# Opening loads on two queues, and the bias products moved behind the fourth slice of a hybrid decoder layer

## The chip, the core and the metric

The kernel is one program on one core of a Trainium2 chip. The core has five engines with instruction streams of their own: TensorE (PE in the profile) multiplies, VectorE (DVE) and ScalarE (ACT) work elementwise, GpSimd (POOL) helps with copies, and SyncE (SP) mostly issues transfers. Transfers are moved by 16 DMA engines; SP, ACT and POOL can each issue them. The metric is the device time in microseconds (us) of one execution, as the median of several.

## What is computed

One layer of a decoder for 256 tokens of width 1024, all in float32. The parts that matter here, cut from the reference and shortened:

```python
h = jnp.einsum('bsd,de->bse', x, w_in[l])
qa, ka, va, za, qb, kb, vb, zb, ga, gb = _split_cols(h)
ya = swa_sink_attention(qa, ka, va, sinks[l], table_a) * jax.nn.silu(za)   # window 128
yb = moba_attention(qb, kb, vb, table_b) * jax.nn.silu(zb)                 # one block of 256
...
bias = rel_table.astype(jnp.float32)[t5_bucket(dist)]     # added to the attention logits
...
merged = sigmoid(ga + b) * (ya @ w_out_a) + sigmoid(gb + b) * (yb @ w_out_b)
x = layer_norm(DN_ALPHA * x + merged @ w_out, ln_gamma[l], ln_beta[l])
```

Each of the 16 heads adds to its logits a bias that depends only on the distance of query and key. The distance is put into one of 32 buckets, and the bias is the entry of a 32x16 table for this bucket and head.

## The kernel before

**Products in two parts.** A float32 operand is split into a high part, rounded to the one-pass format `fp32r`, and the rest (`xh`, `xl` for the input, `wh`, `wl` for weights). A product is high by high, low by high and high by low. So each weight tile is loaded (`wraw`, SP's queue), rounded by ACT into `wh` (L138), subtracted by DVE into `wl` (L153), and used by PE. There are five `wraw` buffers, so a load waits until DVE has finished the `wl` of the tile five before it; a load also waits for the transfer issued eight before it to land.

**Stages.** PE first runs nine warm-up products on constants (L65). Then come the value projections in eight slices k = 0 to 7 of the contraction (L313 to L318): slice k needs 128 rows of the input (`xraw`, 128 KB) and 320 KB of `w_v`, and PE does 12 products of 320 columns with them: four with `wh` and `xh`, four with `wh` and `xl`, four with `wl` and `xh`. After the slices come the projection tiles of `w_t`, 512 KB each, called here t0, t1, t2 and so on: t0 is the keys of the first branch, t1 to t4 its queries, then the second branch, gates and output. A head pair's scores follow its queries: the logits stand in a PSUM bank, DVE adds the bias and takes the row's extreme (L235, L248), ACT takes exponentials (L250), DVE normalises (L263 to L270), and PE transposes and applies the values.

**The bias.** A product of the table (`tab`, 32 rows, each head's column repeated 16 times) with a 0/1 matrix (`oh`, 32 rows, which bucket each distance has) gives for 128 partitions the bias along all distances. There are two such products, one per branch (L323). DVE copies each in reversed order into `rvec` (L324), POOL writes it to a scratch `rd` in device memory (L325), and SP reads it back skewed, as `toep`, 16 transfers of 128 KB (L120), two of them ahead of each of the tiles t2, t3 and t4, and so on. In `rd` and `toep` the halves are the branches: the first eight transfers of `toep` need only the first write. The first products with the table stand after slice 0.

**What sets the order.** It is written by hand: a list `order` of tiles is walked by two cursors, `fetch` (the load and ACT's rounding) and `split` (DVE's subtraction), which run two and one tiles ahead of PE in the slices, and further later. Each engine, and each queue, works in program order. So whatever stands on SP behind a `toep` transfer waits until this can be issued.

Of the kernel before, what the change touches and what calls it, by code (L numbers as in the profile page):

```python
# [11 lines left out]
F32 = mybir.dt.float32  # L12
F32R = mybir.dt.float32r
BF16 = mybir.dt.bfloat16
AF = mybir.ActivationFunctionType
ALU = mybir.AluOpType

P = 128
# [4 lines left out]
NB = 32  # L23
# [5 lines left out]
RL = 384  # L29
# [17 lines left out]
def hybrid_layer(ctx: ExitStack, tc: tile.TileContext, xT, x2, w_t, w_v, w_a, w_b, w_o,  # L47
                 b_gate, sinks, table, onehot, gamma, beta, out):
    nc = tc.nc
    const = ctx.enter_context(tc.tile_pool(name="const", bufs=1))  # L50
    wp = ctx.enter_context(tc.tile_pool(name="wp", bufs=1))
    work = ctx.enter_context(tc.tile_pool(name="work", bufs=2))
# [6 lines left out]
    def bank(tag):  # L59
        return psum.tile([P, 512], F32, tag=tag, name=f"ps_{tag}", bufs=banks[tag])  # L60
# [6 lines left out]

    rvec = work.tile([P, 2, RL], F32, tag="pr_", name="rvec", bufs=4)
    nc.gpsimd.memset(rvec, NEG)
    tab = const.tile([NB, 2 * P], F32, name="tab")  # L70
    oh = work.tile([NB, RL], F32, tag="res", name="oh")
    nc.gpsimd.dma_start(tab, table)
    nc.gpsimd.dma_start(oh, onehot)
    sink = const.tile([P, 8], F32, name="sink")
    nc.gpsimd.dma_start(sink, sinks)
    bg = const.tile([P, 16], F32, name="bg")
    nc.gpsimd.dma_start(bg, b_gate)
    ident = const.tile([P, P], F32, name="ident")
    make_identity(nc, ident)
    nsink = const.tile([P, 8], F32, name="nsink")  # L80
    eps = const.tile([P, 1], F32, name="eps")
    nc.gpsimd.memset(eps, LN_EPS)
# [7 lines left out]
    xraw = const.tile([P, NK, S], F32, tag="x8", name="xraw")  # L90
    xh = const.tile([P, NK, S], F32R, name="xh")
# [18 lines left out]
    def quarters(w):  # L110
        return w.rearrange("p (a b) -> p a b", a=4)[:, :, :S]

    def fetch(kind, n):

        if kind == "r":

            for a in (2 * n, 2 * n + 1):
                src = bass.AP(tensor=rd.tensor, offset=rd.offset + (a // 8) * 16 * RW + (a % 8) * RL,
                              ap=[[RW + 8, 16], [1, 8], [1, S]])
                nc.sync.dma_start(toep[:, a, :], src)  # L120
            return
        if kind == "v":
            nc.sync.dma_start(xraw[:, n, :], xT[:, n, :])
            nc.scalar.activation(xh[:, n, :], xraw[:, n, :], AF.Copy)
        width = 640 if kind == "v" else 1024
        src = {"v": lambda: w_v[:, n, :], "t": lambda: w_t[n], "a": lambda: w_a[n], "b": lambda: w_b[n],
               "o": lambda: w_o[n * P:(n + 1) * P, :]}[kind]()
        raw = wp.tile([P, 1024], F32, tag="raw", name="wraw", bufs=RAWS)
        wh = wp.tile([P, 4 * OW], F32R, tag="wh", name="wh", bufs=8)
        parts = 2 if (kind, n) == ("v", 0) else 1  # L130
        cuts = [slice(i * width // parts, (i + 1) * width // parts) for i in range(parts)]
        for cut in cuts:
            nc.sync.dma_start(raw[:, cut], src[:, cut])
        if kind == "o":
            nc.scalar.activation(quarters(wh), raw.rearrange("p (a b) -> p a b", a=4), AF.Copy)
        else:
            for cut in cuts:
                nc.scalar.activation(wh[:, cut], raw[:, cut], AF.Copy)  # L138
        raws[kind, n] = raw, wh, width

    def split(kind, n):

        if kind == "r":
            return
        if kind == "v":
            nc.vector.tensor_sub(xl[:, n, :], xraw[:, n, :], xh[:, n, :].bitcast(F32))
        raw, wh, width = raws.pop((kind, n))
        wl = wp.tile([P, 4 * OW], F32R, tag="wl", name="wl", bufs=8)
        if kind == "o":
            nc.vector.tensor_sub(quarters(wl), raw.rearrange("p (a b) -> p a b", a=4), quarters(wh).bitcast(F32))  # L150
            nc.vector.tensor_reduce(sums[:, n:n + 1], raw[:, 3 * S:], axis=mybir.AxisListType.X, op=ALU.add)
        else:
            nc.vector.tensor_sub(wl[:, :width], raw[:, :width], wh[:, :width].bitcast(F32))  # L153
        ready[kind, n] = wh, wl

    cursors = [0, 0]

    def advance(stage, at, far):
        at += 1
        while at < len(order) and far:  # L160
            far -= order[at][0] != "r"
            at += 1
        while cursors[stage] < at:
            (fetch, split)[stage](*order[cursors[stage]])
            cursors[stage] += 1
# [7 lines left out]
    def weights(kind, n):  # L173
        lead(kind, n)
        return ready[kind, n]
# [137 lines left out]
    for k in range(NK):  # L313
        wh, wl = weights("v", k)
        for a, w, s0, s1 in ((xh, wh, k == 0, False), (xl, wh, False, False), (xh, wl, False, k == NK - 1)):
            for c in range(2):
                for t in range(2):
                    nc.tensor.matmul(vacc[t][c], a[:, k, t * P:(t + 1) * P], w[:, c * 320:(c + 1) * 320],  # L318
                                     start=s0, stop=s1)
        if k == 0:  # L320
            for s, (lo, hi) in enumerate(REACH):
                pr = bank("pt")[:, :hi - lo]
                nc.tensor.matmul(pr, tab[:, s * P:(s + 1) * P], oh[:, s * P:s * P + hi - lo], start=True, stop=True)  # L323
                nc.vector.tensor_copy(rvec[:, s, TOP + 1 - hi:TOP + 1 - lo], pr[:, ::-1])  # L324
                nc.gpsimd.dma_start(rd[s].rearrange("(p l) -> p l", p=P), rvec[:, s, :])  # L325
            nc.gpsimd.tensor_scalar_mul(nsink, sink, -1.0)
# [19 lines left out]
    for i in range(12):  # L346
# [15 lines left out]
        if 1 <= i < 9:  # L362
            n = i - 1
# [10 lines left out]
    for br, (tiles, w_y) in enumerate(((GA, "a"), (GB, "b"))):  # L374
        for c in range(8):
# [9 lines left out]
            else:  # L385
                m = work.tile([P, S], F32, name="m")
# [27 lines left out]
    for t in range(2):  # L414
        ts = slice(t * P, (t + 1) * P)
        res = work.tile([P, D], F32, tag="res", name="res")
# [64 lines left out]
        cuts = [(0, 448), (448, 832), (832, D)]  # L481
        for (lo, hi), queue in zip(cuts, (nc.sync, nc.sync, nc.scalar)):
            cut = slice(lo, hi)
# [73 lines left out]
```

## Time and profile before

| | |
|---|---|
| median of 3 runs | 198.87 us (198.54 to 199.08) |
| the profiled execution's own time | 198.86 us |
| its span, first to last instruction | 197.1 us |
| busy: PE, DVE, ACT, POOL | 188.0, 136.7, 112.5, 44.1 us |
| moved by DMA | 37.43 MB, mean 190 GB/s |
| SP's queue, share of the 16 DMA engines' span | 57.4% |
| mean granted TensorE clock | 0.99 |

Times in the trace are counted from the span's start. A row of the timeline gives the start and the length in us, the engine (SPq is SP's sequencer issuing a transfer), the line, the operation, what it writes and reads, and in brackets the idle time of the engine before it with what ended this. In a row of windows each engine's busy time is followed by its number of instructions, then come the clock, the mean busy share of the DMA engines and GB/s. The busy time of PE says little, since its products are pipelined; its idle times say more.

### The profile page before, as it was taken

The page shows a single profiled execution, that of the slowest core. Times are in us where ns is not written, and L with a number is a line of the kernel's source. Part 1 is how long each engine was busy: PE and PEld are TensorE (multiplying, and loading weights), DVE is VectorE, ACT ScalarE, POOL GpSimd, SP SyncE. Part 2 cuts the span into 40 slices and gives each one's busy share as a digit, 9 for nine tenths or more (in the row PEclk, how much of TensorE's full clock was granted, in tenths as well). Part 3 has the DMA queues.
Part 4 walks back from the last instruction along what each step waited for, and adds up shares of the span by engine and source line. Part 5 has one row for each costly group of instructions (what it writes and reads, how often), then busy time and mean ns, then how long its engine had stood idle before and what let it go on. Part 6 is the DMA issues. An engine that isn't in the chain of part 4 may idle for free.

```text
span 197.1 us, 3919 instructions
## 1 busy us (share of the span) xinstructions
PE 188.0 (95%) x1469; PEld 178.0 (90%) x1469; DVE 136.7 (69%) x280; ACT 112.5 (57%) x223; POOL 44.1 (22%) x89
## 2 busy tenths in 40 slices
PE   8999999699999999999999999999999999999970
PEld 3799999599999999989999999999999999888860
DVE  0596277987897796686777547447585878696873
ACT  5575757479679669766679444246554746540110
POOL 7020043456599683100000000000000000004230
PEclk9999999999999999999999999999999999999996
DMA  5999999774363454044667865474847499400202
GB/s 139 306 400 346 266 288 318 193 249 149 120 195 126 122 147 166 7 150 170 209 209 234 299 221 152 170 224 145 288 145 266 139 323 334 170 0 0 104 3 106
DMA packets 14082, 37.43 MB, mean 190 GB/s; under 512 B 1632, under 2 KB 5744, under 8 KB 14064
## 3 DMA queue, kind: packets, MB, share of 16 engines
q1 hardware_dynamic: 13520, 36.51, 57.4%
q0 software_dynamic: 256, 0.49, 0.7%
q8 instruction: 11, 0.18, 0.4%
q10 hardware_dynamic: 288, 0.20, 0.3%
q14 instruction: 7, 0.06, 0.1%
HBM read 35.75 MB, written 1.44 MB: 189 GB/s over the span
## 4 chain that ended last, share of the span: by engine, by line
PE 77%; DMA 13%; DVE 4%; SPq 1%; issue 1%; ACT 1%; DVEq 0%; ACTq 0%
PE ps_acc L181 19%; PE ps_acc L182 19%; PE ps_acc L184 19%; PE ps_acc L424 6%; DMA wraw<-in_w_v 5%; DMA wraw<-in_w_t 5%; PE ps_sc L424 4%; DMA toep<-rd 4%; PE ps_pt L281 3%; PE ps_o L300 2%; DVE wl L153 2%; PE ps_sc L241 2%; PE ps_pt L424 1%; PE ps_sc L233 1%; PE ps_o L302 1%
## 5 line engine op out<-in xcount | busy, mean ns | idle before, releaser
L181 PE MATMUL ps_acc<-xh,wh 128*128 128x256 f32 x296 | 71.7, 281 | 0.0
L182 PE MATMUL ps_acc<-xl,wh 128*128 128x256 f32 x296 | 71.4, 280 | 0.0
L153 DVE TENSOR_TENSOR wl<-wraw,wh 128x1024 fp32r<-128x1024 f32 (+1 forms) x53 | 61.2, 1170 | 5.4 <-ACT wh L138 4.3
L138 ACT ACTIVATE wh<-wraw 128x1024 fp32r<-128x1024 f32 (+2 forms) x54 | 52.7, 989 | 8.4 <-DMA wraw<-in_w_t 5.0
L181 PEld LDWEIGHTS ps_acc<-xh,wh 128*128 128x128 f32 x296 | 55.8, 189 | 0.2 <-issue 0.2
L182 PEld LDWEIGHTS ps_acc<-xl,wh 128*128 128x128 f32 x296 | 55.8, 188 | 0.0
L184 PE MATMUL ps_acc<-xh,wl 128*128 128x256 f32 x296 | 41.0, 281 | 0.7 <-DVE wl L153 0.7
L184 PEld LDWEIGHTS ps_acc<-xh,wl 128*128 128x128 f32 x296 | 37.5, 188 | 0.9 <-DVE wl L153 0.9
L412 POOL CAST wh<-sums 128x2 fp32r<-128x2 f32 x8 | 1.5, 182 | 93.7 <-ACT sums L408 93.7
L379 ACT ACTIVATE sg<-ps_acc,bg 128x256 f32<-128x256 f32 x16 | 7.6, 475 | 19.3 <-PE ps_acc L184 19.2
L181 PE MATMUL ps_acc<-yh,wh 128*128 128x256 f32 x64 | 15.8, 281 | 0.0
L182 PE MATMUL ps_acc<-yl,wh 128*128 128x256 f32 x64 | 15.8, 280 | 0.0
L200 POOL CAST kall<-kall 64x512 fp32r<-64x512 f32 x10 | 10.7, 1065 | 14.9 <-DVE kall L198 14.3
L384 DVE TENSOR_TENSOR ga<-ps_acc,sg 128x256 f32<-128x256 f32 x8 | 3.4, 424 | 13.9 <-ACT wh L138 13.9
L181 PEld LDWEIGHTS ps_acc<-yh,wh 128*128 128x128 f32 x64 | 12.1, 188 | 0.0
L182 PEld LDWEIGHTS ps_acc<-yl,wh 128*128 128x128 f32 x64 | 12.0, 188 | 0.0
L389 ACT ACTIVATE mm<-m 128x256 fp32r<-128x256 f32 x8 | 3.4, 419 | 12.0 <-DVE m L388 12.0
L184 PE MATMUL ps_acc<-yh,wl 128*128 128x256 f32 x64 | 10.1, 279 | 0.0
L150 DVE TENSOR_TENSOR wl<-wraw,wh 128x1024 fp32r<-128x1024 f32 x8 | 9.7, 1218 | 0.1
L198 DVE TENSOR_TENSOR kall<-ps_acc,kall 64x256 fp32r<-64x256 f32 x10 | 4.2, 423 | 7.6 <-ACT kall L196 7.5
L424 PE MATMUL ps_acc<-wh,mm 128*128 128x512 f32 x32 | 8.8, 396 | 0.0
L184 PEld LDWEIGHTS ps_acc<-yh,wl 128*128 128x128 f32 x64 | 8.6, 188 | 0.0
(177 smaller groups left out, 302.6 us busy)
## 6 DMA issues: line engine op xcount, KB each, us to landing
wraw<-in_w_t SPq DMA_DIRECT2D x37, 512.0 KB, 3.9
wraw<-in_w_o SPq DMA_DIRECT2D x8, 512.0 KB, 5.0
wraw<-in_w_v SPq DMA_DIRECT2D x7, 320.0 KB, 5.3
toep<-rd SPq DMA_DIRECT2D x16, 128.0 KB, 7.0
wraw<-in_w_a SPq DMA_DIRECT2D x4, 512.0 KB, 3.3
wraw<-in_w_b SPq DMA_DIRECT2D x4, 512.0 KB, 4.5
xraw<-in_xT SPq DMA_DIRECT2D x8, 128.0 KB, 5.1
xr<-in_x SPq DMA_DIRECT2D x1, 1024.0 KB, 8.0
```

What stands on the lines that cost most here:

```text
L138: nc.scalar.activation(wh[:, cut], raw[:, cut], AF.Copy)
L150: nc.vector.tensor_sub(quarters(wl), raw.rearrange("p (a b) -> p a b", a=4), quarters(wh).bitcast(F32))
L153: nc.vector.tensor_sub(wl[:, :width], raw[:, :width], wh[:, :width].bitcast(F32))
L181: nc.tensor.matmul(acc, wh[:, cols[k]], ah[:, a0 + k, :], start=(k == 0), stop=False)
L182: nc.tensor.matmul(acc, wh[:, cols[k]], al[:, a0 + k, :], start=False, stop=False)
L184: nc.tensor.matmul(acc, wl[:, cols[k]], ah[:, a0 + k, :], start=False, stop=(k == n - 1))
L198: nc.vector.tensor_sub(l[r, j, :], acc[r, :], h[r, j, :].bitcast(F32))
L200: nc.gpsimd.tensor_copy(kall[halves[1 - j], b, :, j, :], kall[r, b, :, j, :])
L241: nc.tensor.matmul(o[:, j, :], q[:, j, P:], kall[:, b, part, j, :], start=(j == 0 and part == 0), stop=(j == 1 and part == 1))
L281: nc.tensor.transpose(pt[:, b * P:(b + 1) * P], pr[:, j, b * P:(b + 1) * P], ident)
L379: nc.scalar.activation(sg, acc, AF.Sigmoid, bias=bg[:, at:at + 1])
L424: nc.tensor.matmul(acc, a[:, k, ts], w[:, q:q + n, :cols], start=s0, stop=s1)
```

## The change

Three things are changed, all in the first 15 us of the program.

1. **The opening loads.** Slice 0's input, the two halves of its weights, and slice 1's input were issued on SP's queue in this order: input 0, weights 0 first half, weights 0 second half, input 1. Now SP issues input 0 and the second half of weights 0, and ACT's queue issues the first half and input 1, ahead of all of ACT's work. All later loads stay on SP.
2. **The bias products.** Table and 0/1 matrix are loaded twice, one copy in rows 0 to 31 and one in rows 32 to 63 of the same tiles. The table is split: rows 0 to 31 of `split_tab` hold its high part, rows 32 to 63 the rest. The 0/1 matrix is copied into `places` in the format `fp32r`, by POOL. A product over 64 rows then adds high part and rest in one pass of `fp32r`, instead of a float32 product over 32 rows. The two products, DVE's copies into `rvec` and POOL's writes to `rd` follow slice 3 instead of slice 0.
3. **The small loads** (table, 0/1 matrix, sinks, gate bias) are still issued by POOL, six of them instead of four.

```diff
+    tab = const.tile([2 * NB, 2 * P], F32, name="tab")
+    oh = work.tile([2 * NB, RL], F32, tag="res", name="oh")
+    split_tab = work.tile([2 * NB, 2 * P], F32R, tag="m", name="split_tab")
+    places = work.tile([2 * NB, RL], F32R, tag="pts", name="places", bufs=4)
+    for dst, src in ((tab, table), (oh, onehot)):
+        for r in rows:
+            nc.gpsimd.dma_start(dst[r, :], src)
...
     make_identity(nc, ident)
+    nc.gpsimd.tensor_copy(places, oh)
...
+        if (kind, n) == ("v", 0):
+            nc.sync.dma_start(xraw[:, 0, :], xT[:, 0, :])
+            nc.scalar.dma_start(raw[:, cuts[0]], src[:, cuts[0]])
+            nc.sync.dma_start(raw[:, cuts[1]], src[:, cuts[1]])
+            nc.scalar.dma_start(xraw[:, 1, :], xT[:, 1, :])
+        else:
+            if kind == "v" and n > 1:
+                nc.sync.dma_start(xraw[:, n, :], xT[:, n, :])
+            nc.sync.dma_start(raw[:, :width], src)
+        if kind == "v":
+            nc.scalar.activation(xh[:, n, :], xraw[:, n, :], AF.Copy)
...
+        if (kind, n) == ("v", 2):
+            nc.scalar.activation(split_tab, tab, AF.Copy)
...
+        if (kind, n) == ("v", 2):
+            nc.vector.tensor_sub(split_tab[rows[1], :], tab[rows[1], :], split_tab[rows[1], :].bitcast(F32))
...
-        if k == 0:
+        if k == 3:
             for s, (lo, hi) in enumerate(REACH):
                 pr = bank("pt")[:, :hi - lo]
-                nc.tensor.matmul(pr, tab[:, s * P:(s + 1) * P], oh[:, s * P:s * P + hi - lo], start=True, stop=True)
+                nc.tensor.matmul(pr, split_tab[:, s * P:(s + 1) * P], places[:, s * P:s * P + hi - lo], start=True, stop=True)
                 nc.vector.tensor_copy(rvec[:, s, TOP + 1 - hi:TOP + 1 - lo], pr[:, ::-1])
                 nc.gpsimd.dma_start(rd[s].rearrange("(p l) -> p l", p=P), rvec[:, s, :])
```

Lines below L67 stand 6 to 17 lines further down in the changed kernel: slices L335, bias products L340, copies L341, writes to `rd` L342, `toep` L126, loads L137 to L144, ACT's rounding L151, DVE's subtraction L168.

SP's program from its start, before, with the transfers that it waits for (DMAHW are the eight counters that SP's and ACT's transfers take in turn; a wait on one means that the transfer issued eight before has landed):

```order
L123 DMA xraw<-in_xT 128x256
L133 DMA wraw<-in_w_v 128x320 x2
L123 DMA xraw<-in_xT 128x256
L133 DMA wraw<-in_w_v 128x640
L123 DMA xraw<-in_xT 128x256
```

SP now:

```order
L137 DMA xraw<-in_xT 128x256
L139 DMA wraw<-in_w_v 128x320
L144 DMA wraw<-in_w_v 128x640
L143 DMA xraw<-in_xT 128x256
L144 DMA wraw<-in_w_v 128x640
```

The full weights of slice 1 (128x640) have moved from the fifth place on SP to the third; the other two transfers stand on ACT, ahead of its table load.

DVE's program around the copies of the bias, before (`xl` and `wl` are the rests of a slice's input and weights; the first two rows belong to slice 1):

```order
L146 TENSOR_TENSOR xl<-xraw,xh 128x256
L153 TENSOR_TENSOR wl<-wraw,wh 128x640
L324 COPY rvec<-ps_pt 128x128
L324 COPY rvec<-ps_pt 128x256
L146 TENSOR_TENSOR xl<-xraw,xh 128x256
L153 TENSOR_TENSOR wl<-wraw,wh 128x640
```

DVE now, from the third `wl` on:

```order
L168 TENSOR_TENSOR wl<-wraw,wh 128x640
L170 TENSOR_TENSOR split_tab<-tab,split_tab 32x256
L161 TENSOR_TENSOR xl<-xraw,xh 128x256
L168 TENSOR_TENSOR wl<-wraw,wh 128x640
L161 TENSOR_TENSOR xl<-xraw,xh 128x256
L168 TENSOR_TENSOR wl<-wraw,wh 128x640
L341 COPY rvec<-ps_pt 128x128
L341 COPY rvec<-ps_pt 128x256
L161 TENSOR_TENSOR xl<-xraw,xh 128x256
```

The copies have moved from behind slice 1's `wl` to behind slice 4's, since DVE runs one slice ahead of PE; a subtraction for the table has come in behind slice 2's.

SP's program where the bias is read back, now (it reads the same before but for the lines and counters; the two tiles ahead are t0 and t1, the one between the pairs is t2, the last is t3; DMASW6 is the first write to `rd`):

```order
L144 DMA wraw<-in_w_t 128x1024 [waits DMAHW1_49,DVE_49]
L144 DMA wraw<-in_w_t 128x1024 [waits DMAHW2_49,DVE_49]
L126 DMA toep<-rd 128x1x256 [waits DMAHW3_49,DMASW6_49]
L126 DMA toep<-rd 128x1x256 [waits DMAHW4_49]
L144 DMA wraw<-in_w_t 128x1024 [waits DMAHW5_49,DVE_49]
L126 DMA toep<-rd 128x1x256 [waits DMAHW6_49]
L126 DMA toep<-rd 128x1x256 [waits DMAHW7_49]
L144 DMA wraw<-in_w_t 128x1024 [waits DMAHW0_49,DVE_49]
```

Here nothing has moved: the place in SP's queue is as before, while the write that its third row waits for now follows slice 3.

More of the change, by code (lines that the diff above doesn't have):

```diff
@@ L69, in hybrid_layer @@
     nc.gpsimd.memset(rvec, NEG)
[L70 to L73, printed above, removed]
+    rows = [slice(i * NB, (i + 1) * NB) for i in range(2)]
+    tab = const.tile([2 * NB, 2 * P], F32, name="tab")
[5 more added lines that the diff above has]
+            nc.gpsimd.dma_start(dst[r, :], src)
     sink = const.tile([P, 8], F32, name="sink")
@@ L121, in fetch @@
             return
-        if kind == "v":
-            nc.sync.dma_start(xraw[:, n, :], xT[:, n, :])
-            nc.scalar.activation(xh[:, n, :], xraw[:, n, :], AF.Copy)
         width = 640 if kind == "v" else 1024
@@ L131, in fetch @@
         cuts = [slice(i * width // parts, (i + 1) * width // parts) for i in range(parts)]
-        for cut in cuts:
-            nc.sync.dma_start(raw[:, cut], src[:, cut])
+        if (kind, n) == ("v", 0):
[9 more added lines that the diff above has]
+            nc.scalar.activation(xh[:, n, :], xraw[:, n, :], AF.Copy)
         if kind == "o":
```

## The prediction

> **What bounds the kernel now.** I read the page first, its busy times by engine.
>
> ```profile
> PE 188.0 (95%) x1469; PEld 178.0 (90%) x1469; DVE 136.7 (69%) x280; ACT 112.5 (57%) x223; POOL 44.1 (22%) x89
> ```
>
> PE is busy almost throughout, so the question is where it isn't. The table of waits for PE in the first 60 us (total, times, longest):
>
> ```profile
> PE ps_sc L233 <- DVE nm L248: 0.9, 1, 0.9
> ...
> PE ps_acc L184 <- DVE wl L153: 0.7, 1, 0.7
> PE ps_acc L318 <- ACT wh L138: 0.4, 1, 0.4
> ```
>
> After its start PE loses 0.4 us ahead of slice 1, and 0.7 and 0.9 near 36 and 39 us. From 40 us the rest of its program runs without a gap to 188 us. So the time moves by as much as PE's place at 40 us moves, and a gain earlier than 36 us is kept only if the two later waits don't grow by it. What ends them is the third view, the timeline, picked along one chain:
>
> ```profile
> 28.81 1.06 ACT L138 ACTIVATE wh<-wraw 128x1024 fp32r<-128x1024 f32 x1 [1.08 <-DMA wraw<-in_w_t]
> ...
> 29.90 0.39 ACT L215 ACTIVATE qh<-ps_acc 128x256 fp32r<-128x256 f32 x1
> ...
> 30.32 0.42 DVE L216 SCALAR_TENSOR_TENSOR ql<-ps_acc,qh 128x256 fp32r<-128x256 f32 x1 [0.42 <-ACT qh L215]
> ...
> 34.92 2.55 DVE L153 TENSOR_TENSOR wl<-wraw,wh 128x1024 fp32r<-128x1024 f32 x2
> ...
> 36.19 1.21 PE L184 MATMUL ps_acc<-xh,wl 128*128 128x256 f32 x8 [0.74 <-DVE wl L153]
> ...
> 38.95 0.74 PE L233 MATMUL ps_sc<-kall,q 128*128 128x256 f32 x2 [0.90 <-DVE nm L248]
> ```
>
> ACT sat idle 1.08 us until the load of t4 landed at 28.8, and only then rounded t4 and t2's queries (29.90), which stand behind it on ACT. DVE goes from these queries through the first softmax to `wl` of t4 at 34.92, and PE waits for it at 36.19. The chain has no slack: **the landing of t4 sets PE's place at 40 us.** And t4 comes late because the DMA engines have no room, as the windows show (the last two figures are DMA share and GB/s):
>
> ```profile
> 2.00:8.00 6.00, 5.80 (x23) 3.40 (x21) 1.68 (x3) 2.34 (x6) 2.31 (x7) 1.00 0.87 248
> 8.00:16.00 8.00, 7.78 (x53) 7.78 (x54) 7.07 (x14) 5.86 (x13) 1.51 (x3) 1.00 1.04 393
> 16.00:18.30 2.30, 2.30 (x18) 2.30 (x17) 1.16 (x2) 1.68 (x2) 0.00 (x0) 1.00 1.09 349
> 18.30:24.00 5.70, 5.70 (x47) 5.70 (x46) 2.45 (x2) 3.62 (x8) 0.00 (x0) 1.00 1.05 271
> 24.00:34.00 10.00, 10.00 (x87) 10.00 (x87) 6.96 (x19) 6.29 (x17) 3.70 (x6) 1.00 1.05 295
> ```
>
> From 8 to 34 us the share is full; only 2 to 8 us has holes.
>
> **Part one, the opening loads.** These rows of the timeline carry it:
>
> ```profile
> 0.76 4.00 PE L65 MATMUL ps_o<-const-bfloat16-1.0 128*128 128x512 bf16 x9 [0.76 <-PEq L547]
> ...
> 1.16 0.89 SPq L133 DMA_DIRECT2D wraw<-in_w_v  x2
> ...
> 2.57 0.43 SPq L133 DMA_DIRECT2D wraw<-in_w_v  x1
> ...
> 3.26 0.42 ACT L124 ACTIVATE xh<-xraw 128x256 fp32r<-128x256 f32 x1 [1.25 <-DMA xraw<-in_xT]
> ...
> 4.50 0.63 PE L318 MATMUL ps_acc<-wh,xh 128*128 128x320 f32 x1
> ...
> 6.88 0.92 PE L323 MATMUL ps_pt<-oh,tab 32*128 32x128 f32 x4
> ...
> 7.44 0.74 ACT L138 ACTIVATE wh<-wraw 128x640 fp32r<-128x640 f32 x1 [0.82 <-DMA wraw<-in_w_v]
> ...
> 8.22 0.42 PE L318 MATMUL ps_acc<-wh,xh 128*128 128x320 f32 x1 [0.42 <-ACT wh L138]
> ...
> 10.08 0.31 PE L318 MATMUL ps_acc<-wh,xh 128*128 128x320 f32 x1
> ...
> 13.60 0.30 PE L318 MATMUL ps_acc<-wh,xh 128*128 128x320 f32 x1
> ```
>
> Slice 0 begins at 4.50, and PE's queue holds nine warm-up products until about then (0.76 plus 4.00), so I expect no gain there. Slice 1's weights are issued at 2.57, two issues of 0.47 earlier in the change: 0.94 us is the upper bound of the gain, nothing the lower. Between them lies what the holes allow: 6 us at 0.13 idle are 0.78 us, and the second copies of table and 0/1 matrix (32 and 48 KB, 82 kB in all) take 0.33 us at 248 GB/s. I take the difference, **0.45 us**, as the gain of slice 1 (8.22) and all slices behind it, so slice 3 ends at 13.60 - 0.45 = 13.15. ACT's two issues fit into its idle time ahead of 3.26 us, where input 0 lands.
>
> The Trainium skill's page "DMA: Bandwidth & Descriptors" (Issuing engines are not separate DMA queues) says that transfers from several engines share the same 16 DMA engines, and that a second issuer saves only the sequencer's time. The full share from 8 us on agrees; the holes ahead of it leave room, and no row before can tell how much. If the rule holds strictly this part gives nothing, which is the fourth case below.
>
> **Part two, the bias products.** The old ones took 0.92 us (6.88 to 7.80), but PE then waited 0.42 us more for slice 1, so taking them away frees nothing beyond part one. The new ones are two passes of at most 256 columns. The nearest prices, one row each of the chain of waits, of the groups by form (twice), of the timeline and of the transfers:
>
> ```profile
> 46.98 0.47 PE ps_sc L241 x4
> ...
> L208 ACT ACTIVATE q<-ps_acc 64x256 fp32r<-64x256 f32 x2 | 0.8, 380 | 0.0
> ...
> L200 POOL CAST kall<-kall 64x512 fp32r<-64x512 f32 x10 | 10.7, 1065 | 14.9 <-DVE kall L198 14.3
> ...
> 2.15 0.51 POOL L73 DMA_DIRECT2D oh<-in_onehot  x1
> ...
> oh<-in_onehot POOLq DMA_DIRECT2D x1, 48.0 KB, 3.6
> ```
>
> L241 took 0.12 us for one product of that size, so **0.24 us** on PE, now on the path (0.92 at most, if 64 rows ran like the old 32). Slice 4 begins at 13.15 + 0.24 = 13.39, 0.21 us earlier than now. ACT's rounding of the table is 0.38 us and DVE's subtraction about the same, against 0.6 us of copies that leave the same stretch of DVE; both are covered, since slices pass ACT and DVE in 1.2 us and PE in 1.76 (three and a half microseconds for the two from 10.08 to 13.60). Uncovered they would cost 0.4 us each. POOL issues two more loads of 0.5 us, so the last 0/1 copy is issued near 3.2 and lands near 6.8; its cast, under 1.07 us, is done before 8, well ahead of 13.15. What else stands behind on POOL (sinks, gate bias, identity) is used far later.
>
> **What the move makes late** is the write to `rd`, for which SP waits. The rows are of the timeline, and between them the landing times of POOL's line 325:
>
> ```profile
> 8.95 0.62 DVE L324 COPY rvec<-ps_pt 128x128 f32<-128x128 f32 x2
> ...
> 9.53 1.10 POOL L325 DMA_DIRECT2D rd<-rvec  x2 [5.14 <-DVE rvec L324]
> ...
> DMA to landing us min/median/max: 4.8/4.9/5.1
> ...
> 11.90 1.51 SPq L133 DMA_DIRECT2D wraw<-in_w_t  x2
> ...
> 14.32 1.26 SPq L120 DMA_DIRECT2D toep<-rd  x2
> 15.67 0.54 SPq L133 DMA_DIRECT2D wraw<-in_w_t  x1
> ```
>
> Now the first write is issued at 9.53 and lands 4.8 us later; SP, done with t0 and t1 at 13.41, waits 0.9 us and issues `toep` at 14.32, t2 at 15.67. In the change: products done at 13.39; about 0.26 us from PE to a reader, as from the end of t0 (22.52 plus 1.11) to ACT's next row:
>
> ```profile
> 22.52 1.11 PE L184 MATMUL ps_acc<-xh,wl 128*128 128x256 f32 x8
> ...
> 23.89 0.76 ACT L196 ACTIVATE kall<-ps_acc 64x256 fp32r<-64x256 f32 x2
> ```
>
> so DVE copies at 13.65, and the write is issued 0.58 us later (8.95 to 9.53), at 14.2. Its landing is the first disputed number: 4.8 us as now would be 19.0; 3.6, as the 0/1 matrix took on an emptier chip, 17.8. SP has then stopped feeding, so less traffic competes; I take 4.1, **18.3 us**, four microseconds later than 14.32. All that SP has queued by then (input, slices, t0, t1, the writes, small loads) is 5.3 MB; the windows sum to 5.5 MB by 18.3, the holes filled add 0.1, so the engines run dry shortly before, for some 1 to 2 us.
>
> From there to the landing of t4 stand six `toep` of 131 kB and three tiles of 524 kB, 2.36 MB. A `toep` lands at best 3.1 us after its issue (landing times of SP's line 120):
>
> ```profile
> DMA to landing us min/median/max: 3.1/7.0/8.3
> ```
>
> and the other 2.23 MB take 7.6 us at 295 GB/s or 8.2 at 271. So t4 lands at 18.3 + 3.1 + 7.9 = 29.3 against 28.8 now, SP's nine issues of 0.6 us being quicker than this. The sum: **+0.5 us at ACT's wait**, and along the chain to 36.19 and 38.95. PE's lead of 0.21 us is swallowed there. I round down to +0.4, since t4 also needs fewer transfers in flight beside it than now (`toep` then sat behind a full queue): 198.86 + 0.4 = **199.3 us**, with 1.76 us outside the span as before. The profiled execution's 198.86 is the median's 198.87, so nothing is shifted. 0.3%, what a measurement of this kernel can tell from no change, is 0.6 us.
>
> The bounds: with 0.94 us of gain and 3.6 us of landing `toep` starts at 17.3 and t4 lands at 28.0; with no gain and 4.8 us at 19.4 and 30.7. On the early side there is a floor: t2's queries can't be rounded before PE is through with t2:
>
> ```profile
> 28.21 1.10 PE L184 MATMUL ps_acc<-xh,wl 128*128 128x256 f32 x8
> ```
>
> 29.31 plus 0.26, against 29.90 now, and less by what PE leads, 0.2 to 0.7 us: at most 0.5 to 1.0 us can be won.
>
> **The rivals.** *Slower, by SP's stop.* The second write to device memory and the restart cost what they cost now: landing at 4.8 us, then 271 GB/s. `toep` at 19.0, t4 at 19.0 + 3.1 + 8.2 = 30.3, +1.5: about 200.2 us. For it: 4.8 to 5.1 is the only time that these writes showed. Against it: they then shared the engines with SP's full queue. It decides from `toep` issued after about 18.5. *Faster.* The front gains 0.94, the writes land in 3.6 us, the dry stretch is short and tiles come without a backlog: t4 lands ahead of 28.2 and PE's own progress sets the chain: -0.7, 198.2 us. For it: the waits at 36 and 39 hang on DMA, so they may shrink too. Against it: `toep` has to be issued by 17.3. *The second queue does nothing.* Slice 1 stays at 8.22, the products at 13.60, `toep` at 18.75, t4 at 29.7: +0.9, 199.8 us. The share of 0.87 in the holes speaks against it; that slice 1's weights, issued at 2.57, had ACT waiting until 7.44, most of it spent behind other transfers, speaks for it.
>
> **How the numbers follow.** My forecast has 0.48 (0.38 of it within 0.3%, 0.10 slower), the slower rival 0.20, the faster one 0.20 (0.18 beyond 0.3%), the idle second queue 0.12 (0.10 slower). Together 0.18 faster, 0.42 the same, 0.40 slower. The range of 198.2 to 200.4 reaches from the faster rival to just past the slower one and leaves out the extremes of both bounds; the forecast's own is 198.8 to 199.9.
>
> **What would show it.** In the changed kernel: slice 1's first product near 7.8 and the products of the bias near 13.2, at 0.12 us a pass; SP's wait ahead of the first `toep` at about 5 us in place of 0.8, ending near 18.3; a window near 18 to 20 us with a DMA share well under 1; ACT's rounding of t4 at 29.3; PE's wait at `wl` of t4 above 0.74. I am wrong if `toep` is issued before 17 us, if the DMA share shows no dip, or if PE's wait near 36 shrinks.

## The result, and the profile after

The changed kernel takes 201.38 us (median of 4 runs, 201.09 to 201.59) against 198.77 us before: a ratio of 1.0129, 95% interval 1.0109 to 1.0149. It is slower by 2.6 us, outside the range of 198.2 to 200.4. The profiled execution took 201.29 us (198.86 before). The page's busy times and PE's waits in the first 60 us:

```profile
PE 188.4 (94%) x1467; PEld 177.5 (89%) x1467; DVE 137.0 (69%) x281; ACT 112.5 (56%) x224; POOL 46.0 (23%) x92
```

```profile
PE ps_acc L335 <- ACT wh L151: 1.2, 2, 0.9
PE ps_acc L201 <- DVE wl L168: 1.0, 2, 0.8
PE ps_sc L250 <- DVE nm L265: 0.9, 1, 0.9
PE ps_o L65 <- PEq L564: 0.8, 1, 0.8
PE ps_sc L250 <- DVE q L227: 0.7, 1, 0.7
```

PE's busy time is that of before to 0.4 us; its waits have grown, also by a new one, for the first queries (`q`, L227). SP's waits, the landing of the two writes to `rd` (line 342), and the windows by stage and by microsecond show where from:

```profile
SPq L126 <- DMA rd<-rvec: 5.1, 1, 5.1
```

```profile
DMA to landing us min/median/max: 4.4/4.5/4.5
```

```profile
2.00:8.00 6.00, 4.80 (x20) 2.52 (x18) 1.62 (x4) 3.28 (x7) 3.23 (x8) 1.00 0.97 275
8.00:16.00 8.00, 8.00 (x52) 7.68 (x53) 6.98 (x14) 6.37 (x13) 2.66 (x5) 1.00 1.06 358
16.00:18.30 2.30, 2.30 (x18) 2.30 (x17) 2.13 (x4) 1.21 (x2) 0.00 (x0) 1.00 0.78 307
18.30:24.00 5.70, 5.70 (x46) 5.70 (x45) 1.97 (x2) 2.49 (x5) 0.00 (x0) 1.00 0.54 156
24.00:34.00 10.00, 9.02 (x73) 8.47 (x72) 5.28 (x9) 4.96 (x8) 3.13 (x5) 1.00 1.02 310
```

```profile
18.00:19.00 1.00, 1.00 (x9) 1.00 (x8) 1.00 (x1) 0.48 (x1) 0.00 (x0) 1.00 0.30 120
19.00:20.00 1.00, 1.00 (x9) 1.00 (x8) 0.44 (x2) 0.58 (x1) 0.00 (x0) 1.00 0.00 0
20.00:21.00 1.00, 1.00 (x9) 1.00 (x8) 0.84 (x1) 0.22 (x1) 0.00 (x0) 1.00 0.38 114
21.00:22.00 1.00, 1.00 (x11) 1.00 (x10) 0.00 (x0) 1.00 (x4) 0.00 (x0) 1.00 1.06 171
22.00:23.00 1.00, 1.00 (x11) 1.00 (x10) 0.00 (x0) 0.21 (x1) 0.00 (x0) 1.00 0.47 141
23.00:24.00 1.00, 1.00 (x11) 1.00 (x10) 0.00 (x0) 0.00 (x0) 0.00 (x0) 1.00 0.98 395
```

SP stands for 5.1 us ahead of the first `toep` (0.8 before), and the DMA engines run dry: nothing moves from 19 to 20 us, and the share from 18.3 to 24 is 0.54 where it was 1.05. The timeline, first the opening and the bias, then the chain at 30 us:

```profile
4.77 0.42 ACT L146 ACTIVATE xh<-xraw 128x256 fp32r<-128x256 f32 x1 [1.84 <-DMA xraw<-in_xT]
...
5.59 0.41 PE L335 MATMUL ps_acc<-wh,xh 128*128 128x320 f32 x1 [0.91 <-ACT wh L151]
...
7.99 0.42 PE L335 MATMUL ps_acc<-wh,xh 128*128 128x320 f32 x1 [0.29 <-ACT wh L151]
```

```profile
9.75 1.11 POOL L85 CAST places<-oh 64x384 fp32r<-64x384 f32 x1 [4.45 <-DMA oh<-in_onehot]
...
13.22 0.31 PE L335 MATMUL ps_sc<-wl,xh 128*128 128x320 f32 x1
...
13.46 0.49 PE L340 MATMUL ps_pt<-places,split_tab 64*128 64x128 f32 x2
...
13.88 0.41 PE L335 MATMUL ps_acc<-wh,xh 128*128 128x320 f32 x1
...
14.41 1.11 POOL L342 DMA_DIRECT2D rd<-rvec  x2 [3.51 <-DVE rvec L341]
...
18.92 1.26 SPq L126 DMA_DIRECT2D toep<-rd  x2
...
20.27 0.54 SPq L144 DMA_DIRECT2D wraw<-in_w_t  x1
...
24.88 1.06 ACT L151 ACTIVATE wh<-wraw 128x1024 fp32r<-128x1024 f32 x1 [2.67 <-DMA wraw<-in_w_t]
```

```profile
28.40 1.06 ACT L151 ACTIVATE wh<-wraw 128x1024 fp32r<-128x1024 f32 x1 [1.81 <-DMA wraw<-in_w_t]
...
30.85 0.82 PE L250 MATMUL ps_sc<-kall,q 128*128 128x256 f32 x2 [0.72 <-DVE q L227]
...
31.32 1.06 ACT L151 ACTIVATE wh<-wraw 128x1024 fp32r<-128x1024 f32 x1 [1.06 <-DMA wraw<-in_w_t]
...
32.40 0.38 ACT L232 ACTIVATE qh<-ps_acc 128x256 fp32r<-128x256 f32 x1
...
37.41 2.55 DVE L168 TENSOR_TENSOR wl<-wraw,wh 128x1024 fp32r<-128x1024 f32 x2
...
38.68 1.21 PE L201 MATMUL ps_acc<-xh,wl 128*128 128x256 f32 x8 [0.84 <-DVE wl L168]
...
41.44 0.74 PE L250 MATMUL ps_sc<-kall,q 128*128 128x256 f32 x2 [0.90 <-DVE nm L265]
```

The first input is rounded at 4.77 (3.26 before), so slice 0 begins at 5.59 (4.50), and slice 1, at 7.99, is 0.23 us earlier than before. t4 is rounded at 31.32 against 28.81, and each step of the chain behind it is 2.5 us later: t2's queries 32.40 (29.90), `wl` of t4 37.41 (34.92), PE's product 38.68 (36.19), the scores 41.44 (38.95). The profiled executions differ by 2.43 us. The whole loss is there by 41 us.

### The profile page after: what moved, and what is told of

Its sections match the earlier page's. It is cut to its first block, busy times and chain, and to the rows that moved or that the text cites. A ratio compares the mean times of both kernels' runs of the same rounds, so it can differ in the third digit from the quotient of the medians.

```text
span 199.5 us, 3921 instructions
## 1 busy us (share of the span) xinstructions
PE 188.4 (94%) x1467; PEld 177.5 (89%) x1467; DVE 137.0 (69%) x281; ACT 112.5 (56%) x224; POOL 46.0 (23%) x92
## 4 chain that ended last, share of the span: by engine, by line
PE 79%; DMA 10%; SPq 4%; DVE 4%; issue 1%; ACT 1%; DVEq 0%; ACTq 0%
PE ps_acc L198 19%; PE ps_acc L199 19%; PE ps_acc L201 19%; PE ps_acc L441 6%; DMA wraw<-in_w_t 5%; PE ps_sc L441 4%; DMA wraw<-in_w_v 3%; PE ps_pt L298 3%; SPq L126 2%; DMA rd<-rvec 2%; PE ps_o L317 2%; PE ps_sc L258 2%; PE ps_acc L335 1%; PE ps_pt L441 1%; PE ps_sc L335 1%
## 5 line engine op out<-in xcount | busy, mean ns | idle before, releaser
L168 DVE TENSOR_TENSOR wl<-wraw,wh 128x1024 fp32r<-128x1024 f32 (+1 forms) x53 | 61.1, 1169 | 3.1 <-ACT wh L151 2.9
L151 ACT ACTIVATE wh<-wraw 128x1024 fp32r<-128x1024 f32 (+2 forms) x54 | 52.5, 987 | 9.2 <-DMA wraw<-in_w_t 6.8
L201 PE MATMUL ps_acc<-yh,wl 128*128 128x256 f32 x64 | 10.1, 279 | 0.0
```

Of the source, the lines that this page charges most:

```text
L201: nc.tensor.matmul(acc, wl[:, cols[k]], ah[:, a0 + k, :], start=False, stop=(k == n - 1))
```

## The experiments

The theory: SP stands still until the bias is in device memory, the DMA engines run dry behind it, and PE follows the landing of t4. The rivals: the opening itself costs, as its first input comes late; or the second copies of the small loads do. Ratios are to runs of the kernel before on the same chip, with 95% intervals.

**Each part alone.** First the two queues alone; the bias as before:

```diff
-        if kind == "v":
-            nc.sync.dma_start(xraw[:, n, :], xT[:, n, :])
...
-        for cut in cuts:
-            nc.sync.dma_start(raw[:, cut], src[:, cut])
+        if (kind, n) == ("v", 0):
+            nc.sync.dma_start(xraw[:, 0, :], xT[:, 0, :])
+            nc.scalar.dma_start(raw[:, cuts[0]], src[:, cuts[0]])
+            nc.sync.dma_start(raw[:, cuts[1]], src[:, cuts[1]])
+            nc.scalar.dma_start(xraw[:, 1, :], xT[:, 1, :])
...
```

> Only the opening loads are split over SP's and ACT's queues; the bias products stay as before, behind slice 0 and in 32 rows. Theory (SP stands still until the bias has been written to device memory, and t4's landing moves with it): the write to rd is issued within 0.5 us of 9.53, the first toep near 14.3, so the time stays within 0.5 us of before, 198.4 to 199.3. Rival (the split makes the first input late, rounded at 4.77 in the changed kernel against 3.26, and that is what costs): most of the 2.6 us is here, 200.5 to 201.5.

Measured 198.94 us, ratio 1.0021 (0.9992 to 1.0051). Its timeline has the late first input, and an early `toep`:

```profile
4.31 0.42 ACT L140 ACTIVATE xh<-xraw 128x256 fp32r<-128x256 f32 x1 [1.39 <-DMA xraw<-in_xT]
...
14.44 1.26 SPq L120 DMA_DIRECT2D toep<-rd  x2
```

So with the second queue alone input 0 is rounded 1.05 us later. The time doesn't tell whether this costs anything: the interval reaches to 0.5%, 1 us, far from the 2.6. Next only the place of the products, in 32 rows and with the old loads:

```diff
-        if k == 0:
+        if k == 3:
             for s, (lo, hi) in enumerate(REACH):
```

> Only the place of the bias products is changed, from behind slice 0 to behind slice 3; loads on SP's queue and 32-row products as before. Theory: the first toep is issued near 18.5 to 19, DMA engines run dry near 19 us, and t4 is rounded 2 to 2.5 us later; 200.6 to 201.5. Rival (opening loads): the write leaves later, but nothing is lost but the 0.9 us of products on PE; at most 199.3.

Measured 200.51 us, ratio 1.0096 (1.0061 to 1.0131), 1.8 us of the 2.6 and just under the 200.6 that I expected. SP's first `toep` and the window behind it:

```profile
18.90 1.26 SPq L120 DMA_DIRECT2D toep<-rd  x2
```

```profile
18.30:24.00 5.70, 5.70 (x44) 5.70 (x43) 2.75 (x3) 2.49 (x5) 0.00 (x0) 1.00 0.56 173
```

Nearly the same stop (4.8 us) and the same dry window as in the changed kernel, with the opening untouched. t4 is rounded at 30.21, 1.4 us later than before, where I expected 2 to 2.5. Then the whole change of the bias with the old opening; the diff is against the changed kernel:

```diff
+        if kind == "v":
+            nc.sync.dma_start(xraw[:, n, :], xT[:, n, :])
...
-        if (kind, n) == ("v", 0):
-            nc.sync.dma_start(xraw[:, 0, :], xT[:, 0, :])
-            nc.scalar.dma_start(raw[:, cuts[0]], src[:, cuts[0]])
...
+        for cut in cuts:
+            nc.sync.dma_start(raw[:, cut], src[:, cut])
...
```

> The whole change of the bias (two copies of the small loads, one-pass products of 64 rows behind slice 3), with the opening loads all on SP as before. Theory: as the changed kernel within 0.6 us, 200.8 to 201.8, with the first toep near 18.7. Rival (opening loads): 198.5 to 199.3. A third reading, that the second copies of the small loads crowd the opening by themselves, is shown if input 0 is rounded later than 3.5 us here too.

Measured 201.23 us, ratio 1.0123 (1.0102 to 1.0145): the loss of the changed kernel without its second queue.

```profile
3.23 0.42 ACT L130 ACTIVATE xh<-xraw 128x256 fp32r<-128x256 f32 x1 [1.23 <-DMA xraw<-in_xT]
```

Its first input is rounded at 3.23 us, so the second copies of the small loads don't delay that one; its first `toep` is issued at 19.26.

**The stop taken away.** Now the changed kernel with `toep` later on SP's queue, so that the same work is there, but t2 and t3 stand ahead of the wait:

```diff
     for t in range(GA):
         order += [("t", t)]
-        if QA <= t < KQB:
-            order.append(("r", t - QA))
-        elif KQB < t < ZA and (t - KQB) % 2:
-            order.append(("r", 4 + (t - KQB) // 2))
+        if QA <= t - 2 < KQB:
+            order.append(("r", t - 2 - QA))
+        elif KQB < t - 2 < ZA and (t - 2 - KQB) % 2:
+            order.append(("r", 4 + (t - 2 - KQB) // 2))
```

> The changed kernel, but each pair of toep transfers stands two tiles later on SP's queue, so that t2 and t3 are issued ahead of the first pair and SP has nothing to wait for. Theory: the dry stretch of the DMA engines near 19 us goes, t4 lands before 29 us, and the time falls to 197.8 to 199.0. Rival (opening loads or the small loads): the loss stays, 200.8 to 201.8.

Measured 198.65 us, ratio 0.9997 (0.9973 to 1.0022): all of it is back, though the writes to `rd` and the first `toep` (19.68) are as late as ever, and SP still stands 2.6 us for them. Rows of ACT and PE:

```profile
27.79 1.06 ACT L151 ACTIVATE wh<-wraw 128x1024 fp32r<-128x1024 f32 x1
...
36.09 1.21 PE L201 MATMUL ps_acc<-xh,wl 128*128 128x256 f32 x8 [0.19 <-DVE wl L168]
```

t4 is rounded at 27.79 and PE waits 0.19 us at 36.09 where it waited 0.84 at 38.68. The edit also takes two pairs of `toep` from ahead of t4. In the kernel before, which has no long stop to take away, the same edit (shown below) brings t4 from 28.81 to 27.59 and leaves the time as it was. So the loss lies in what SP's stop holds back, not in the late bias and not in the opening. With one tile in place of two (`t - 1` for `t - 2`), SP still stops, but behind t2:

> The changed kernel with each pair of toep transfers one tile later. SP still stops until the first write has landed near 19 us, but t2 is queued ahead of the stop, 524 kB or 1.3 us of transfers more, and lands before PE needs it. Theory: about half of the loss comes back, t3 is the first late tile, 199.2 to 200.3. Rival (what costs is not the stop but the late toep itself): 200.8 or more.

Measured 198.90 us, ratio 1.0011 (0.9986 to 1.0036): more came back than the half that I expected.

```profile
19.00 1.26 SPq L126 DMA_DIRECT2D toep<-rd  x2
...
28.49 1.06 ACT L151 ACTIVATE wh<-wraw 128x1024 fp32r<-128x1024 f32 x1 [0.80 <-DMA wraw<-in_w_t]
...
29.73 0.38 ACT L232 ACTIVATE qh<-ps_acc 128x256 fp32r<-128x256 f32 x1 [0.18 <-PE ps_acc L201]
```

`toep` starts at 19.00, but only two tiles are behind it, t4 is rounded at 28.49, and t2's queries at 29.73 wait for PE, no longer for a load. SP's wait for the write was shorter here, since it issued t2 in the meantime:

```profile
SPq L126 <- DMA rd<-rvec: 3.1, 1, 3.1
```

The DMA share still falls to 0.42 from 20 to 21 us. So with one tile more ahead of it, a stop of 3.1 us costs nothing that these runs can tell, even where the engines run low.

**From what lateness it costs.** The kernel before with its 32-row products behind slice 1 (`k == 1`):

> The kernel before with the 32-row products behind slice 1 in place of slice 0. Theory with a point from which it decides (the loss begins when the engines run dry, near 17.4 us, and what is queued covers an earlier stop): the first toep is issued near 16 to 16.5, the engines never run dry, t4 moves by under 0.7 us, 198.7 to 199.4. Rival (loss in proportion to the lateness of toep, 1.8 us for 4.6): 0.7 us or more, 199.4 to 199.9.

Measured 199.29 us, ratio 1.0022 (0.9998 to 1.0045), unclear. Its timeline and the window that ran dry elsewhere:

```profile
15.24 1.26 SPq L120 DMA_DIRECT2D toep<-rd  x2
...
30.20 0.38 ACT L215 ACTIVATE qh<-ps_acc 128x256 fp32r<-128x256 f32 x1 [0.53 <-PE ps_acc L184]
```

```profile
18.30:24.00 5.70, 5.70 (x45) 5.70 (x45) 2.45 (x2) 4.50 (x7) 0.00 (x0) 1.00 0.97 273
```

`toep` came at 15.24, earlier than I expected; the DMA share stays at 0.97, and ACT waits 0.53 us for PE ahead of t2's queries. So no dry stretch formed, and the 0.4 us, if real, are on PE's side, where 0.92 us of products then stand between slices 1 and 2. From what lateness a stop costs, this run doesn't show: its `toep` came only 0.92 us later than before and not near the 17.4 us that I had reckoned.

**Is there something to gain?** The kernel before with `toep` two tiles later:

> The kernel before with each pair of toep transfers two tiles later on SP's queue, nothing else. Theory (t4's landing sets PE's place at 40 us): t2, t3 and t4 land earlier, ACT rounds t2's queries as soon as PE has them (29.6 in place of 29.9), PE's wait at t4 falls from 0.74 to 0.2 to 0.5; 198.0 to 198.6. Rival (the toep transfers are then late for the first scores): t4 is early, but DVE waits for toep after 31 us and the time grows to 199.0 or more.

Measured 198.75 us, ratio 0.9990 (0.9970 to 1.0009), above the 198.0 to 198.6 of the theory. The rows are as the theory has them:

```profile
29.60 0.39 ACT L215 ACTIVATE qh<-ps_acc 128x256 fp32r<-128x256 f32 x1 [0.95 <-PE ps_acc L184]
...
35.89 1.21 PE L184 MATMUL ps_acc<-xh,wl 128*128 128x256 f32 x8 [0.19 <-DVE wl L153]
```

ACT waits for PE ahead of t2's queries (29.60 against 29.90), and PE reaches t4's last products 0.30 us earlier. The gain stands in the profiled execution and is too small to be told in the times. Two further attempts to add to it, the second queue (as in the first experiment) and the loads of sinks and gate bias moved behind the writes to `rd`:

```diff
-    nc.gpsimd.dma_start(sink, sinks)
-    nc.gpsimd.dma_start(bg, b_gate)
...
                 nc.gpsimd.dma_start(rd[s].rearrange("(p l) -> p l", p=P), rvec[:, s, :])
+            nc.gpsimd.dma_start(sink, sinks)
+            nc.gpsimd.dma_start(bg, b_gate)
```

> The kernel before with the opening loads on two queues and toep two tiles later; bias products as before. Theory: as the one without the second queue within 0.3 us, since the opening moves PE's start of slice 2 by less than 0.3 us and PE waits at 36 us anyway; 198.0 to 198.8. Rival (an earlier opening is worth something once SP never stops): 197.2 to 197.9.

> The kernel before with toep two tiles later, and with the loads of sinks and gate bias (128 rows of 32 and 64 bytes each) issued by POOL behind the writes to rd in place of the opening. Theory (these loads crowd the opening, where 4 to 5 us moved 157 GB/s at a share of 0.82): slice 1 begins 0.2 to 0.5 us before 8.22, PE's floor at 36 us moves with it, 198.0 to 198.5. Rival (no gain in the opening survives the chain at 36 us): 198.6 to 198.9.

Measured 198.81 us, ratio 1.0003 (0.9977 to 1.0029), and 198.47 us, ratio 0.9993 (0.9970 to 1.0015). Neither is faster than the kernel before. In the second, slice 1 began at 8.45, not earlier than 8.22, so these two loads weren't what held the opening. That its median lies in the theory's range is therefore no support for the theory.

**Why t4 came so late after the stop.** From the first `toep` to t4's rounding the changed kernel took 12.4 us (18.92 to 31.32), where I had reckoned 11.0 from bytes and rates. It moved more than stood ahead of t4:

```profile
18.90:31.30 12.40, 11.43 (x89) 10.88 (x88) 4.51 (x8) 5.63 (x11) 2.10 (x2) 1.00 0.82 244
```

12.4 us at 244 GB/s are 3.0 MB, against 2.36. One buffer for weights less (`RAWS = 4`) keeps t6 back:

> The changed kernel with four buffers for loaded weights in place of five, so that the load of t6 can't be issued before DVE is through with t2, near 29 us, and t5 not before t1's. Measured in the changed kernel: from the first toep (18.92) to t4's rounding (31.32) 12.4 us, in which 3.0 MB were moved, though only 2.36 MB stand ahead of t4. Theory (transfers issued behind t4 are moved beside it and delay it): without t6 the 12.4 us fall to 10.5 to 11.7. Rival (each toep and the restart are slow by themselves): they stay at 12.2 or more. The whole time is not predicted well, since t1 comes later too: 200.5 to 202.

Measured 201.82 us, ratio 1.0150 (1.0122 to 1.0178), and the first `toep` to t4 took 13.2 us. The issue of the second `toep` took 1.41 us there (0.63 for the first), so the fair stretch is from t2's issue:

```profile
21.09 0.53 SPq L144 DMA_DIRECT2D wraw<-in_w_t  x1
...
32.13 1.06 ACT L151 ACTIVATE wh<-wraw 128x1024 fp32r<-128x1024 f32 x1 [1.02 <-DMA wraw<-in_w_t]
```

11.04 us, against 11.05 in the changed kernel (20.27 to 31.32). t6 was issued only near 30.7 and this changed nothing: that t6 delays t4 isn't borne out. A pair of `toep` and t5 still stood right behind t4, so what all the traffic behind it costs is not shown. The other suspect is `toep` itself. The scratch is read with a skew, each row of 1 KB starting at another multiple of 4 bytes. Read straight (with a bias that isn't the reference's):

```diff
-                src = bass.AP(tensor=rd.tensor, offset=rd.offset + (a // 8) * 16 * RW + (a % 8) * RL,
-                              ap=[[RW + 8, 16], [1, 8], [1, S]])
+                src = bass.AP(tensor=rd.tensor, offset=rd.offset + (a // 8) * 16 * RW,
+                              ap=[[RW, 16], [RL, 8], [1, S]])
```

> The changed kernel, but toep reads the scratch without the skew, rows of 1 KB that begin every 1.5 KB, so the bias added is not the reference's and only the time counts; transfers, bytes and waits are the same. Disputed is why t4 comes 12.4 us after the first toep and not 11.0. Theory A (the skewed reads, which begin at any multiple of 4 bytes, are dear in the engines: 171 GB/s at a share of 1.06 at 21 to 22 us): t4 is rounded at most 11.3 us after the first toep, and the time falls by 0.8 us or more to 200.5 or less. Theory B (the restart and the queue's depth): 12 us or more, time within 0.5 us of 201.4.

> The same change of the toep reads in the kernel before, again with a bias that is not the reference's. Theory A: the tiles t2 to t4 follow one another in less than 2.5 us in place of 2.9, t4 lands before 28.3, and PE's floor at 29.6 for t2's queries limits the gain to 0.3 us: 198.3 to 198.8. Theory B: t2 to t4 still 2.9 us apart, 198.5 to 199.0.

The changed kernel so altered took 199.70 us, ratio 1.0063 (1.0044 to 1.0082), and its t4 came 10.1 us after the first `toep`:

```profile
18.79 0.88 SPq L126 DMA_DIRECT2D toep<-rd  x2
...
28.91 1.06 ACT L151 ACTIVATE wh<-wraw 128x1024 fp32r<-128x1024 f32 x1 [0.16 <-DMA wraw<-in_w_t]
```

The kernel before so altered took 198.44 us, ratio 0.9990 (0.9961 to 1.0018), with this window (18.3 to 24 had 271 GB/s before):

```profile
18.30:24.00 5.70, 5.70 (x45) 5.70 (x45) 1.91 (x2) 3.10 (x6) 0.00 (x0) 1.00 1.05 385
```

Read with the skew, the engines moved 271 GB/s at the same share of busy time as 385 GB/s straight. In the kernel before this is hidden, since PE's own floor is near; t2's queries then wait for PE:

```profile
30.06 0.38 ACT L215 ACTIVATE qh<-ps_acc 128x256 fp32r<-128x256 f32 x1 [0.95 <-PE ps_acc L184]
```

Behind the dry stretch it is not hidden: of the changed kernel's 1.29% of loss 0.63% are left (0.44 to 0.82), so about half goes with the skewed reads, some 1.3 us, and about half stays with the stop. The edit changes two things at once, though. Skewed, a transfer reads 16 groups of eight rows that start 4 bytes apart, so the eight overlap almost wholly; straight, its 128 rows don't overlap, and each starts at a multiple of 1.5 KB. Whether the starts or the overlap are dear was not tested. The Trainium skill's page "DMA: Bandwidth & Descriptors" (How a descriptor splits into AXI transactions) says that a read has to start at a 256-byte boundary, so that an unaligned row fetches bytes that it doesn't use. The direction agrees; by its count a row of 1 KB has five pieces instead of four, a quarter more at most, an estimate. Here it was more: the three pairs of `toep` ahead of t4 took 12.40 - 10.12 = 2.28 us longer skewed than straight (18.92 to 31.32 against 18.79 to 28.91), 0.76 us a pair. Its 262 kB would take 0.67 us in all at the 393 GB/s of the slices, so the skewed read about doubles it, an estimate, where a quarter would be 0.17 us.

## Why the prediction was wrong

**Right: what bounds.** That PE's place at 40 us follows t4's landing, through t2's queries, the first softmax and `wl` of t4, held: t4 +2.5, PE +2.5, the time +2.4 in the profiled executions, and with t4 early again (27.79) the time was that of before.

**Right: the mechanism and its signs in the trace.** SP waits 5.1 us (about 5 foretold), the share has its dip, PE's wait at t4 rose to 0.84, and with two tiles more ahead of the stop the loss is gone. It is the forecast's mechanism, and the rival named "slower, by SP's stop", with a larger size than either had.

**Part one, mis-sized and with a wrong step.** "Slice 0 begins at 4.50, I expect no gain there" missed a loss: it began at 5.59. I had taken the first input to land as before; with a second transfer issued at the same moment it came 1.5 us later (0.4 to 1.5 in the seven kernels with a second queue). Slice 1 gained 0.23 us instead of 0.45. This moved the products by 0.3 us (13.46 for 13.15) and nothing else.

**Part two, mis-sized.** 0.24 us for the two products: slice 3's last product begins at 13.22, slice 4 would have followed 0.15 us later at 13.37 as the other products do, and it began at 13.88, so they cost 0.51. That the small copies are covered was right, though the last 0/1 copy landed near 9.7 and not 6.8 (POOL's cast began at 9.75, under 1.2 us long): these copies took 6.5 us to land, not 3.6.

**The write, nearly right.** Issued at 14.41 (14.2 foretold), landed 4.5 us later (4.1 taken between 3.6 and 4.8), `toep` at 18.92 instead of 18.3. This is 0.6 us of the miss, inside the bounds.

**The step that failed** is the next one, "the other 2.23 MB take 7.6 us at 295 GB/s or 8.2 at 271": 12.4 us from the first `toep` to t4, not 11.0, 1.4 us of the miss. I had taken the rates of windows in which a deep queue was full, and my upper bound used the same rates. Behind an empty queue the engines weren't full: I had reckoned with some 1 to 2 us of dry engines, but the share was 0.30, 0.00 and 0.38 from 18 to 21 us and fell to 0.47 again from 22 to 23, behind the first `toep`. The first group (two `toep` and t2) took 5.96 us to its rounding and the second 3.52, where 2.9 was the pace before; the third was back at 2.92. The skewed reads lengthen the stretch (12.4 us, straight 10.1), but they don't explain the miss by themselves, since the windows that gave 271 and 295 GB/s had such reads in them too. How the 1.4 us divide between the restart and the skew behind an empty queue stays open. Beside it I rounded the sum down by 0.1 us, on the guess that less traffic would be in flight beside t4; the stretch moved 3.0 MB, not the 2.36 of the sum, so nothing bears the rounding out. 0.6 + 1.4 + 0.1 are the 2.1 us between +0.4 and the +2.5 of the chain.

**The rivals.** The sum of the slower one, 198.86 + 1.5, is 200.4 and not the 200.2 that I wrote. That the second queue gives nothing was closer to the truth than my 0.45 us, but its 199.8 us rested on the same rates. The rule weighed there, that a second issuer saves no more than the sequencer's time (the Trainium skill, "DMA: Bandwidth & Descriptors", Issuing engines are not separate DMA queues), agrees with the ratio of the second queue alone, 1.0021 (0.9992 to 1.0051). The faster one needed `toep` by 17.3, and it came at 18.92. The floor for gains held: with t4 early, t2's queries were rounded at 29.60, 0.3 us earlier, and the time didn't move.

**Open** stays why the second group behind the stop took 3.5 us in the changed kernel and 2.3 where only the products were moved (t2 to t3 rounded at 25.11 and 27.45): the latter lost 0.8 us less with nearly the same stop, a difference that the two intervals don't secure.

## What to carry to other kernels

When a producer is moved later, look at what waits for it in a queue that has other work behind the wait: the late datum cost nothing here, the loads queued behind it cost everything, and giving them one place ahead brought it back to within the noise. Estimate what follows a dry queue from the pace of its own transfers, not from the mean rate of full windows, and take strided or skewed transfers apart from plain ones. A second issuing queue for the opening loads delayed the first one, which is the one that is waited for; slice 1's weights came a little earlier (rounded at 6.8 to 7.2 us in the seven kernels with it, at 7.2 to 8.1 in the seven without), and the time showed neither.

## What the runs showed of the hardware

Two things that I had not expected. Issuing a second transfer beside the first one delayed the first: input 0 was rounded at 3.67 to 4.79 us in the seven kernels with two queues and at 3.23 to 3.34 in the seven with one. The doubled small loads don't sort these values: 4.31 and 4.79 are kernels without them, 3.67 to 4.77 kernels with them, and 3.23 is the one with them and one queue. And skewed, overlapping reads of 1 KB rows from device memory kept the DMA engines' share at 1.05 while moving 271 GB/s with the tiles beside them (18.3 to 24 us), where straight rows of the same size moved 385 GB/s in that window at the same share.
